# One division of the attention outputs by transposed inverse sums, in place of a division of each row of probabilities

## The chip, the cores and the metric

The kernel runs on one core of a Trainium2 chip. The metric is the time of one execution on the device, in microseconds (us), as the median of several runs. Each engine of the core (TensorE, VectorE, ScalarE, POOL, also called GpSimd, and SyncE, which only issues transfers) takes its own instructions strictly in order and waits for other engines at semaphores.

## The reference

A trunk of two layers works on 512 latent tokens and 256 context tokens of width 1024. Each layer is a modulated norm, one input projection, four groups of four heads ("mixers"), an output projection, and a SwiGLU feed-forward part. Three of the four mixers are softmax attentions: MLA over all latent and context tokens, a two-dimensional neighbourhood attention (NA) and a windowed attention with sink logits (SWA). The fourth is a retention. Context tokens read only context tokens; in the last layer they are not carried on. Cut to what the change concerns:

```python
def softmax_attend(q, k, v, scale, sink=None):
    s = einsum('bhqd,bhkd->bhqk', q, k) * scale
    if sink is not None:
        s = concatenate([s, broadcast(sink)], axis=-1)
    p = softmax(s, axis=-1)
    if sink is not None:
        p = p[..., :-1]
    return einsum('bhqk,bhkd->bhqd', p, v)
```

The softmax divides each row of exponentials by its sum. Since a row's sum is the same for all of its keys, the division may stand before or behind the product with V.

## The kernel before

**Tiling.** Tokens lie in tiles of 128: four latent, two of context. Attention goes by query tile: six tiles per mixer in the first layer and four in the second, so 3 x 6 + 3 x 4 = 30 query tiles of four heads, 120 heads in all. Widths of a head's row of probabilities P are 768 keys in MLA (32 heads), 512 in NA (32), 512 or 640 in SWA (16 of each) and 256 for context tiles (24).

**One head.** TensorE writes the scores into PSUM (`scores`, line 626, and masks). VectorE takes the row's minimum (the scores are negated; line 1000 and 1002 in MLA). ScalarE writes the exponentials to P in SBUF, with the row's sum as a second result (line 1005 in MLA, in two pieces of 384 keys; lines 1148 and 1150 in SWA, line 939 in NA). `norm_p` (lines 595 to 613) adds the pieces of the sum (line 600 or 604), takes the reciprocal (line 607) and multiplies P by it in place on VectorE (line 613). `attend_T` transposes P in blocks of 128 on TensorE (line 579) and copies the result to SBUF, the first four blocks on ScalarE (line 582), the rest on VectorE (line 584). For each pair of heads `attend_pv` then multiplies V by these (line 592). The output of a tile comes out transposed: features on the partitions, queries along the free dimension, the two pairs in columns 0 to 255 of a PSUM bank of the pool "o". `put` (line 620) copies it to SBUF on ScalarE; for MLA, `merge_mla` instead splits it straight from PSUM into two parts, hi on ScalarE and lo on VectorE (lines 1324 and 1325).

**Queries.** `q_stack` loads a tile of queries, transposes it (line 662), and scales it into two tiles, on ScalarE (line 666) and on VectorE (line 667); the scores need both.

**Around it.** Dense products are computed as three matmuls each (`mm3`, lines 467 to 469), of 128x512 columns near the attention. The order of all instructions comes from a list scheduler, which goes by costs and priorities, and puts dense products between the steps of the attention, so TensorE's listing mixes both. Also in the listing near attention: modulation vectors computed from streamed weights (lines 395 and 397, VectorE), the gating and adding of projections (line 1353 on VectorE, 1355 on POOL), the splitting of weights (line 449 on ScalarE, 213 on VectorE or POOL), the retention's decays (lines 1239 and 1263 on VectorE, 1255 on POOL), and, behind attention, the second norm (line 486 on VectorE, transposed by line 500 on TensorE).

## Time and profile before

| | us |
|---|---|
| median of 3 runs | 1928.17 |
| lowest, highest run | 1925.45, 1930.57 |
| the profiled execution | 1927.69 |
| its span, first to last instruction | 1925.9 |
| TensorE busy | 1832.2 |
| VectorE busy | 1196.8 |
| ScalarE busy | 688.9 |
| POOL busy | 614.3 |

The mean granted clock of TensorE is 0.983 of full speed. The attention lies in four stretches: from about 140 to 303 us (context and latent tiles of NA and SWA, first layer), 438 to 530 (MLA, first layer), 1228 to 1337 (NA and SWA, second layer) and 1450 to 1528 (MLA, second layer). To read the profile, take the busy shares first, then the same per stretch, and then what each wait of the busiest engine ended on: only time for which that engine waits, or which it spends itself, can shorten or lengthen the span directly. In the views of time a row's start is followed by its duration; a duration of several instructions in one row runs from the first start to the last end, and durations of matmuls that follow each other overlap, so the step from one start to the next is what the engine pays.

### The profile page before, as it was taken

To read this page: it belongs to the slowest core of one execution; us is meant where nothing else is said; L and a number is where in the kernel's file an instruction comes from. 1 tells how busy PE (TensorE), PEld (TensorE's weight loads), DVE (VectorE), ACT (ScalarE), POOL (GpSimd) and SP (SyncE) were. 2 spreads that over 40 slices of the span, in tenths; PEclk is the share of its full clock that TensorE was granted. 3 is DMA by queue.
4 is the path that set the end of the run, shared out by engine and by line. 5 is a ranking of instruction groups with operands and counts; after the bars stand their busy time and mean duration, and the time that the engine had idled before them with its cause. 6 is when DMAs were issued, how large, how long until landed. Compare 5 with 4: busy or idle time off the path is not lost.

```text
span 1925.9 us, 32215 instructions
## 1 busy us (share of the span) xinstructions
PE 1832.2 (95%) x12367; PEld 1596.9 (83%) x12367; DVE 1196.8 (62%) x2743; ACT 688.9 (36%) x1597; POOL 614.3 (32%) x573
## 2 busy tenths in 40 slices
PE   7899999899999999999999999899889999999997
PEld 3677776778889989999899978678778899999996
DVE  5796886777898776453334283465588854344336
ACT  3325653255542111222122233464255532222223
POOL 0211113223124553444444121111232145636442
PEclk9999999899999999999999999999999999999998
DMA  7665435453124345342222122422434143223321
GB/s 233 209 205 156 139 98 181 133 167 82 61 83 147 111 153 186 110 136 64 62 67 66 54 97 81 119 73 92 138 111 109 34 125 95 88 88 93 105 77 44
DMA packets 193572, 215.48 MB, mean 112 GB/s; under 512 B 66660, under 2 KB 141578, under 8 KB 193418
## 3 DMA queue, kind: packets, MB, share of 16 engines
q10 hardware_dynamic: 75840, 111.17, 18.3%
q1 hardware_dynamic: 117578, 102.25, 18.0%
q8 instruction: 97, 1.59, 0.3%
q14 instruction: 57, 0.47, 0.1%
HBM read 192.76 MB, written 20.63 MB: 111 GB/s over the span
## 4 chain that ended last, share of the span: by engine, by line
PE 65%; DVE 8%; issue 2%; POOL 2%; DMA 1%; ACT 1%; SPq 0%; ACTq 0%; DVEq 0%; POOLq 0%
PE ps L467 10%; PE ps L468 10%; PE ps L469 10%; PE pg L469 8%; PE pg L467 8%; PE pg L468 8%; PE po L592 2%; PE ps L626 2%; PE pt L579 2%; DVE wl L213 1%; DVE nat L1353 1%; DVE PT L397 1%; DVE P L613 1%; DVE b L1239 1%; DMA qT<-in_ada_w_dram 0%
## 5 line engine op out<-in xcount | busy, mean ns | idle before, releaser
L467 PE MATMUL ps<-b,wh 128*128 128x256 f32 x1760 | 501.9, 285 | 3.8 <-ACT P L1464 3.8
L468 PE MATMUL ps<-b,wh 128*128 128x256 f32 x1760 | 500.9, 285 | 0.0
L469 PE MATMUL ps<-b,wl 128*128 128x256 f32 x1760 | 500.3, 284 | 0.4 <-POOL wl L213 0.4
L467 PE MATMUL pg<-wh,b 128*128 128x512 f32 (+2 forms) x1128 | 441.9, 392 | 1.2 <-ACT b L508 0.9
L469 PE MATMUL pg<-wh,b 128*128 128x512 f32 (+2 forms) x1128 | 440.7, 391 | 0.6 <-POOL b L213 0.6
L468 PE MATMUL pg<-wl,b 128*128 128x512 f32 (+2 forms) x1128 | 439.6, 390 | 1.2 <-DVE rs_yn L288 0.6
L467 PEld LDWEIGHTS ps<-b,wh 128*128 128x128 f32 x1760 | 340.1, 193 | 7.1 <-ACT P L1464 4.1
L468 PEld LDWEIGHTS ps<-b,wh 128*128 128x128 f32 x1760 | 340.1, 193 | 0.8
L469 PEld LDWEIGHTS ps<-b,wl 128*128 128x128 f32 x1760 | 340.2, 193 | 0.6 <-POOL wl L213 0.6
L213 DVE TENSOR_TENSOR wl<-raw,wh 128x1024 fp32r<-128x1024 f32 (+1 forms) x130 | 200.8, 1549 | 199.0 <-ACT wh L449 197.8
L449 ACT ACTIVATE wh<-raw 128x1024 fp32r<-128x1024 f32 (+1 forms) x196 | 202.7, 1049 | 256.9 <-PE pg L469 210.4
L1355 POOL TENSOR_TENSOR b<-b,nat 128x512 f32<-128x512 f32 (+1 forms) x204 | 221.3, 1103 | 114.2 <-DVE nat L1353 81.6
L213 POOL TENSOR_TENSOR wl<-raw,wh 128x1024 fp32r<-128x1024 f32 (+1 forms) x66 | 165.9, 2514 | 265.1 <-ACT wh L449 254.3
L467 PEld LDWEIGHTS pg<-wh,b 128*128 128x128 f32 x1128 | 214.4, 190 | 38.9 <-issue 1.7
L469 PEld LDWEIGHTS pg<-wh,b 128*128 128x128 f32 x1128 | 214.2, 190 | 38.9 <-issue 3.9
L468 PEld LDWEIGHTS pg<-wl,b 128*128 128x128 f32 x1128 | 214.1, 190 | 38.1 <-DVE wl L213 1.7
L1353 DVE TENSOR_TENSOR nat<-pg,gate 128x512 f32<-128x512 f32 x240 | 162.0, 686 | 85.6 <-PE pg L469 80.2
L213 POOL TENSOR_TENSOR b<-P,b 128x256 fp32r<-128x256 f32 x36 | 28.9, 804 | 327.3 <-ACT b L1467 327.3
L1467 ACT ACTIVATE b<-P 128x256 fp32r<-128x256 f32 x110 | 45.7, 416 | 233.0 <-DVE P L1466 221.9
L1466 DVE TENSOR_TENSOR P<-ps,P 128x256 f32<-128x256 f32 x110 | 46.4, 422 | 129.6 <-PE ps L469 129.5
L1464 ACT ACTIVATE P<-ps 128x256 f32<-128x256 f32 x110 | 41.5, 383 | 213.4 <-PE ps L469 131.6
L397 DVE SCALAR_TENSOR_TENSOR PT<-qT,consts,PT 128x512 f32<-128x512 f32 x112 | 102.1, 927 | 19.3 <-DMA qT<-in_ada_w_dram 18.4
(322 smaller groups left out, 2446.5 us busy)
## 6 DMA issues: line engine op xcount, KB each, us to landing
raw<-in_ffn_w_dram ACTq DMA_DIRECT2D x132, 512.0 KB
qT<-in_ada_w_dram ACTq DMA_DIRECT2D x96, 256.0 KB
raw<-in_w_in_dram SPq DMA_DIRECT2D x40, 512.0 KB
a<-in_ada_w_dram SPq DMA_DIRECT2D x32, 256.0 KB
a<-in_ada_w_dram ACTq DMA_DIRECT2D x32, 256.0 KB
xn<-in_ada_w_dram ACTq DMA_DIRECT2D x32, 256.0 KB
raw<-in_w_out_dram SPq DMA_DIRECT2D x16, 512.0 KB
ldq<-q_d SPq DMA_DIRECT2D x40, 128.0 KB
```

What stands on the lines that cost most here:

```text
L213: eng.tensor_tensor(out, full, hi.bitcast(F32), op=ALU.subtract)
L397: dve.scalar_tensor_tensor(acc[s], w, sS[:, k, s:s + 1], acc[s], op0=ALU.mult, op1=ALU.add)
L449: act.activation(hi, raw_ap, AF.Copy)
L467: pe.matmul(ps, a[0], b[0], start=first, stop=False)
L468: pe.matmul(ps, a[0], b[1], start=False, stop=False)
L469: pe.matmul(ps, a[1], b[0], start=False, stop=last)
L579: pe.transpose(ps[:, i * P:(i + 1) * P], Pm[:, (b0 + i) * P:(b0 + i + 1) * P], ident)
L1353: dve.tensor_tensor(tm, ps, gates[(0 if t < 4 else 2) + b], op=ALU.mult)
L1355: eng.tensor_tensor(ap, ap, tm[:, a:c], op=ALU.add)
L1464: act.activation(s1[j][:, sl], ps[:, 0:256], AF.Silu)
L1466: dve.tensor_tensor(s1[j][:, sl], ps[:, 0:256], s1[j][:, sl], op=ALU.mult)
L1467: act.activation(gh[j][:, sl], s1[j][:, sl], AF.Copy)
```

## The change

`norm_p` goes, with its three calls in the mixers and the one in `soft_y` (context tiles). P stays undivided. A new function `inverse` is called once per query tile behind the last product with V: it adds the pieces of the sums for all four heads at once (none, one or two additions of 128x4), takes one reciprocal 128x4, spreads it on POOL to 128x256 (each head's inverse 64 times along the free dimension, into a new SBUF tag `rcb` with two buffers), and transposes this in two blocks on TensorE into columns 256 to 511 of the outputs' PSUM bank, where each inverse then stands at the feature and query at which it is needed. `put` copies the transposed inverses to SBUF on ScalarE and multiplies the outputs by them on VectorE. `merge_mla` goes through `put` into a tile `o` first, and splits hi and lo from there.

```diff
--- before.py
+++ after.py
@@ -75,7 +75,7 @@
 
 
 
-CHANGED = {'pad': {'raw': 1024}, 'bufs': {'raw': 4}}
+CHANGED = {'pad': {'raw': 1024, 'rcb': 256}, 'bufs': {'raw': 4, 'rcb': 2}}
 
 
 def merged(opts):
@@ -592,32 +592,32 @@
                 pe.matmul(pv[64 * e:64 * e + 64, hp * P:hp * P + P], vs[e][i], PTs[e][:, i, :],
                           start=(i == n - 1), stop=(i == 0), tile_position=(0, 64 * e))
 
-    def norm_p(Pm, sums):
-
-        n = sums.shape[1]
-        if n == 2:
-            t = S("sm", 1)
-            dve.tensor_tensor(t, sums[:, 0:1], sums[:, 1:2], op=ALU.add)
-            sums = t
-        elif n > 2:
-            t = S("sm", 1)
-            dve.tensor_reduce(t, sums, axis=AX.X, op=ALU.add)
-            sums = t
-        rc = S("rc", 1)
-        dve.reciprocal(rc, sums)
-        e = PNE[rr["pn"] % len(PNE)]
-        rr["pn"] += 1
-        if e == "act":
-            act.activation(Pm, Pm, AF.Copy, scale=rc[:, 0:1])
+    def inverse(pv, sums):
+
+
+        n = sums.shape[2]
+        if n == 1:
+            t = sums[:, :, 0]
         else:
-            {"dve": dve, "pool": pool}[e].tensor_scalar(Pm, Pm, rc[:, 0:1], 1.0, op0=ALU.mult, op1=ALU.mult)
+            t = S("sm", 4)
+            dve.tensor_tensor(t, sums[:, :, 0], sums[:, :, 1], op=ALU.add)
+            if n == 3:
+                dve.tensor_tensor(t, t, sums[:, :, 2], op=ALU.add)
+        rc = S("rc", 4)
+        dve.reciprocal(rc, t)
+        rb = T("rcb", [P, H, 64])
+        pool.tensor_copy(rb, rc.unsqueeze(2).to_broadcast([P, H, 64]))
+        for hp in range(2):
+            pe.transpose(pv[:, 256 + hp * P:384 + hp * P], rb[:, 2 * hp:2 * hp + 2].rearrange("p a b -> p (a b)"), ident)
 
     def put(pv, dst):
 
-        src = pv[:, 0:256].rearrange("p (a b) -> p a b", a=2)
+        rt = T("rcb", [P, 256])
+        act.activation(rt, pv[:, 256:512], AF.Copy)
+        src, r = (x.rearrange("p (a b) -> p a b", a=2) for x in (pv[:, 0:256], rt))
         if len(dst.shape) == 4:
-            src = pv[:, 0:256].rearrange("p (a r c) -> p a r c", a=2, r=8)
-        act.activation(dst, src, AF.Copy)
+            src, r = (x.rearrange("p (a r c) -> p a r c", a=2, r=8) for x in (pv[:, 0:256], rt))
+        dve.tensor_tensor(dst, src, r, op=ALU.mult)
 
     def scores(ps, q, k):
 
@@ -647,9 +647,9 @@
                                accum_out=sums[:, h, 0:1])
                 if negsink is not None:
                     act.activation(sums[:, h, 1:2], m[:, h:h + 1], AF.Exp, bias=sk[:, h:h + 1])
-                norm_p(Pm, sums[:, h, 0:1 if negsink is None else 2])
                 PTs.append(attend_T(Pm, 2))
             attend_pv(pv, hp, PTs, [v_of(2 * hp), v_of(2 * hp + 1)])
+        inverse(pv, sums[:, :, 0:1 if negsink is None else 2])
         return pv
 
     def q_stack(src, scale):
@@ -942,10 +942,10 @@
                             PTs, vs = [], []
                         vs.append([Vw[(2 * cb + b) // 3][:, (2 * cb + b) % 3, dsl] for b in range(2)]
                                   + [Vyn[:, b, dsl] for b in range(2)])
-                        norm_p(Pm, sums[:, h:h + 1])
                         PTs.append(attend_T(Pm, 4))
                         if h % 2:
                             attend_pv(pv, h // 2, PTs, vs)
+                    inverse(pv, sums.unsqueeze(2))
                     put(pv, st[:, :, 0:NX].rearrange("p a (r c) -> p a r c", c=64)[:, :, :, 16 * cb:16 * cb + 16])
                 Q["so"].dma_start(oT_d[0:256, :].rearrange("(a p) t -> p a t", p=P)[:, :, 0:ntok], st[:, :, 0:ntok])
 
@@ -1006,10 +1006,10 @@
                                        accum_out=s2[:, h, i:i + 1])
                     if h % 2 == 0:
                         PTs = []
-                    norm_p(Pm, s2[:, h])
                     PTs.append(attend_T(Pm, 6))
                     if h % 2:
                         attend_pv(pv, h // 2, PTs, [vof(h - 1, range(6)), vof(h, range(6))])
+                inverse(pv, s2)
                 return pv
 
             def k_rope(t):
@@ -1152,10 +1152,10 @@
                             if h % 2 == 0:
                                 PTs = []
                             act.activation(s3[:, h, 2:3], m[:, h:h + 1], AF.Exp, bias=sink[:, l, h:h + 1])
-                            norm_p(Pm, s3[:, h])
                             PTs.append(attend_T(Pm, nl + 2))
                             if h % 2:
                                 attend_pv(pv, h // 2, PTs, [vof(h - 1, blks + [4, 5]), vof(h, blks + [4, 5])])
+                        inverse(pv, s3)
                         o = pv
                     put(o, st[:, :, rows(t)])
                 Q["so"].dma_start(oT_d[256:512, :].rearrange("(a p) t -> p a t", p=P)[:, :, 0:ntok], st[:, :, 0:ntok])
@@ -1320,7 +1320,8 @@
         def merge_mla(t, pv):
             tsl = slice((t % 2) * P, (t % 2) * P + P)
             hi, lo = (x[:, 0:2, tsl] for x in m_pair(t // 2, 0))
-            v = pv[:, 0:256].rearrange("p (a b) -> p a b", a=2)
+            v = T("o", [P, 2, P])
+            put(pv, v)
             act.activation(hi, v, AF.Copy)
             dve.tensor_tensor(lo, v, hi.bitcast(F32), op=ALU.subtract)
```

In the changed program TensorE has 60 matmuls more, VectorE 226 instructions fewer, ScalarE 10 more and POOL 30 more. The scheduler's order outside of the attention stretches and what lies next to them is as before. Three places follow, with the names and line numbers of each program's own listing (the changed file's lines below `put` are those of before plus one).

TensorE before, a latent MLA tile of the first layer, two pieces. The first begins at the fourth head's last scores (`ps_5264`), the second holds that head's transposes (`P_5271`); `pg` are dense products, `pt` the transposes, `po` the outputs.

```order
L626 MATMUL ps_5264<-b_920_4033,qT_5132 128x384
L626 MATMUL ps_5264<-b_920_4033,qT_5133 128x384
L626 MATMUL ps_5264<-b_921_4034,qT_5145 128x384
L467 MATMUL pg_5545<-wh_5304,b_1156_5034 128x512
L468 MATMUL pg_5545<-wl_5305,b_1156_5034 128x512
L469 MATMUL pg_5545<-wh_5304,b_1156_5034 128x512
L579 MATMUL pt_5172<-consts,P_5163 128x128 x4
L579 MATMUL pt_5178<-consts,P_5163 128x128 x2
L467 MATMUL pg_5545<-wh_5304,b_1156_5034 128x512
L468 MATMUL pg_5545<-wl_5305,b_1156_5034 128x512
L469 MATMUL pg_5545<-wh_5304,b_1156_5034 128x512
L467 MATMUL pg_5545<-wh_5310,b_1156_5034 128x512
```

The second piece, 19 rows further down:

```order
L592 MATMUL po_5148<-PT_5171,b_922_4035 64x128
L579 MATMUL pt_5248<-consts,P_5239 128x128 x2
L579 MATMUL pt_5254<-consts,P_5239 128x128 x2
L469 MATMUL pg_5545<-wh_5310,b_1156_5034 128x512
L467 MATMUL pg_5562<-wh_5304,b_1162_5073 128x512
L579 MATMUL pt_5280<-consts,P_5271 128x128 x4
L579 MATMUL pt_5286<-consts,P_5271 128x128 x2
L468 MATMUL pg_5562<-wl_5305,b_1162_5073 128x512
```

Between the two pieces stand dense products, the second and third heads' transposes and the first pair's products with V. TensorE in the changed program, the fourth head of a latent MLA tile of the first layer:

```order
L579 MATMUL pt_5149<-consts,P_5145 128x128 x4
L579 MATMUL pt_5155<-consts,P_5145 128x128 x2
L626 MATMUL ps_5165<-b_891_3954,qT_5061 128x384
L467 MATMUL pg_5252<-wh_5208,b_1124_4946 128x512
L468 MATMUL pg_5252<-wl_5209,b_1124_4946 128x512
L469 MATMUL pg_5252<-wh_5208,b_1124_4946 128x512
L467 MATMUL pg_5252<-wh_5208,b_1124_4946 128x512
L468 MATMUL pg_5252<-wl_5209,b_1124_4946 128x512
L469 MATMUL pg_5252<-wh_5208,b_1124_4946 128x512
L467 MATMUL pg_5252<-wh_5214,b_1124_4946 128x512
L468 MATMUL pg_5252<-wl_5215,b_1124_4946 128x512
L579 MATMUL pt_5176<-consts,P_5172 128x128 x3
```

The scores of the fourth head (`ps_5165`) are now followed by eight dense products and then by its transposes (`P_5172`), which stand in two pieces.

VectorE before, the same tile of before, from the first head's sum on:

```order
L600 TENSOR_TENSOR sm_5166<-s_1179_5149 128x1
L1000 TENSOR_REDUCE m_1200_5226<-ps_5227 128x1
L607 RECIPROCAL rc_5168<-sm_5166 128x1
L1000 TENSOR_REDUCE m_1200_5226<-ps_5232 128x1
L613 TENSOR_SCALAR P_5163<-P_5163,rc_5168 128x768
L600 TENSOR_TENSOR sm_5198<-s_1179_5149 128x1
L1002 TENSOR_TENSOR m_1203_5237<-m_1200_5226 128x1
L1000 TENSOR_REDUCE m_1210_5258<-ps_5259 128x1
L607 RECIPROCAL rc_5200<-sm_5198 128x1
L1000 TENSOR_REDUCE m_1210_5258<-ps_5264 128x1
L584 COPY PT_5171<-pt_5178 128x256
L613 TENSOR_SCALAR P_5195<-P_5195,rc_5200 128x768
```

VectorE in the changed program, the tile shown of it above, from the first pair's copies to the product in `put`:

```order
L1002 TENSOR_TENSOR m_1169_5143<-m_1166_5132 128x1
L1000 TENSOR_REDUCE m_1174_5159<-ps_5160 128x1
L584 COPY PT_5148<-pt_5155 128x256
L1000 TENSOR_REDUCE m_1174_5159<-ps_5165 128x1
L1002 TENSOR_TENSOR m_1177_5170<-m_1174_5159 128x1
L603 TENSOR_TENSOR sm_5198<-s_1149_5065 128x4
L607 RECIPROCAL rc_5200<-sm_5198 128x4
L584 COPY PT_5175<-pt_5182 128x256
L1354 TENSOR_TENSOR nat_5265<-pg_5252,gate_4798 128x512
L620 TENSOR_TENSOR o_5269<-po_5064,rcb_5270 128x256
```

Additions, reciprocals and scalings between the reductions are gone; one addition and one reciprocal of four columns stand behind the last minimum, and the product (line 620) behind a dense product's gating.

VectorE before, near 153 us, between the first and the second context tile of NA in the first layer; line 395 takes a streamed weight (`xn`), line 639 reduces context scores:

```order
L613 TENSOR_SCALAR P_1394<-P_1394,rc_1396 128x256
L395 TENSOR_SCALAR ldr_3057<-xn_3042,consts 128x512
L667 SCALAR_TENSOR_TENSOR qT_1418<-pt_1412,qT_1417 128x512
L676 TENSOR_TENSOR nat_1992<-pg_1965,nat_1992 128x2x64
L1109 COPY b_453_1964<-pg_1965 128x128
L397 SCALAR_TENSOR_TENSOR ldr_3057<-xn_3045,consts,ldr_3057 128x512
L639 TENSOR_REDUCE m_296_1423<-ps_1424 128x2
L639 TENSOR_REDUCE m_296_1423<-ps_1454 128x2
```

and in the changed program:

```order
L1109 COPY b_447_1940<-pg_1941 128x128
L667 SCALAR_TENSOR_TENSOR qT_1414<-pt_1408,qT_1413 128x512
L395 TENSOR_SCALAR ldr_2977<-xn_2962,consts 128x512
L620 TENSOR_TENSOR st_1332<-po_1345,rcb_1402 128x2x128
L639 TENSOR_REDUCE m_295_1419<-ps_1420 128x2
L639 TENSOR_REDUCE m_295_1419<-ps_1444 128x2
L397 SCALAR_TENSOR_TENSOR ldr_2977<-xn_2965,consts,ldr_2977 128x512
L607 RECIPROCAL rc_1468<-s_294_1418 128x4
```

The scaled queries (line 667) stood behind line 395 and now stand ahead of it; the reductions of the scores stand behind it in both. TensorE in the changed program, where a tile ends: the last product with V, the two transposes of the inverses (line 611), and the queries of a next tile.

```order
L592 MATMUL po_5064<-PT_5175,b_892_3955 64x128
L592 MATMUL po_5064<-PT_5148,b_892_3955 64x128
L611 MATMUL po_5064<-consts,rcb_5202 128x128 x2
L662 MATMUL pt_5278<-consts,ldq_5275 128x128 x4
L982 MATMUL pt_5291<-consts,ldq_5287 96x128 x4
L467 MATMUL pg_5441<-wh_5208,b_1124_4946 128x512
L626 MATMUL ps_5302<-b_887_3950,qT_5283 128x384
L626 MATMUL ps_5307<-b_887_3950,qT_5283 128x384
```

The two transposes stand directly behind the last product with V in all 30 tiles.

## Rows read from the trace of the kernel before

**Rows 1.** The page, busy time, share of the span, instructions.

```profile
PE 1832.2 (95%) x12367; PEld 1596.9 (83%) x12367; DVE 1196.8 (62%) x2743; ACT 688.9 (36%) x1597; POOL 614.3 (32%) x573
```

**Rows 2.** Busy time by stretch: the sum of the four attention stretches; behind the first's end.

```profile
sum 442.00, PE 429.56 PEld 349.24 DVE 338.45 ACT 250.62 POOL 72.68; mean PE 107.39 PEld 87.31 DVE 84.61 ACT 62.65 POOL 18.17
...
530.00:570.00 40.00, 36.01 (x223) 32.31 (x222) 39.57 (x97) 17.21 (x33) 9.11 (x5) 0.97 0.30 100
```

**Rows 3.** TensorE's waits over the span: total us, times, longest us.

```profile
PE ps L626 <- DVE qT L667: 5.0, 3, 2.7
...
PE pt L500 <- DVE xn L486: 3.7, 2, 2.2
PE pt L579 <- DVE P L613: 3.4, 5, 1.0
...
PE pt L579 <- DVE sm L604: 0.8, 2, 0.4
```

**Rows 4.** TensorE in time, an MLA tile: start us, us, line, operation, count.

```profile
463.50 0.39 PE L467 MATMUL pg<-wh,b 128*128 128x512 f32 x1
463.73 0.39 PE L468 MATMUL pg<-wl,b 128*128 128x512 f32 x1
...
467.54 0.38 PE L579 MATMUL pt<-consts,P 128*128 128x128 f32 x2
467.85 1.53 PE L592 MATMUL po<-PT,b 128*64 128x128 f32 x24
...
470.27 0.82 PE L579 MATMUL pt<-consts,P 128*128 128x128 f32 x6
```

**Rows 5.** Groups by line: count | busy us, mean ns of one | idle before.

```profile
L613 DVE TENSOR_SCALAR P<-P,rc 128x512 f32<-128x512 f32 (+3 forms) x120 | 67.0, 561 | 1.4
L607 DVE RECIPROCAL rc<-sm 128x1 f32<-128x1 f32 x72 | 11.0, 155 | 0.6
L1466 DVE TENSOR_TENSOR P<-ps,P 128x256 f32<-128x256 f32 x110 | 46.4, 422 | 129.6 <-PE ps L469 129.5
...
L620 ACT ACTIVATE st<-po 128x256 f32<-128x256 f32 x20 | 7.7, 385 | 17.3 <-PE po L592 12.7 <-DVE ldr L397 4.6
...
L883 POOL COPY b<-o 128x256 f32<-128x256 f32 x4 | 3.6, 910 | 24.0 <-ACT nat L675 15.1 <-DVE nat L795 6.5 <-DVE o L879 2.3
```

**Rows 6.** VectorE, ScalarE and TensorE in time, from scores to transposes.

```profile
495.17 0.16 DVE L1002 TENSOR_TENSOR m<-m 128x1 f32<-128x1 f32 x1
495.24 0.55 DVE L1000 TENSOR_REDUCE m<-ps 128x1 f32<-128x384 f32 x1
...
495.36 0.58 ACT L1005 ACTIVATE P<-ps,m 128x384 f32<-128x384 f32 x1 [3.21 <-DVE m L1002]
...
495.83 0.16 DVE L1002 TENSOR_TENSOR m<-m 128x1 f32<-128x1 f32 x1
...
495.93 0.57 ACT L1005 ACTIVATE P<-ps,m 128x384 f32<-128x384 f32 x1
...
496.40 0.20 ACT L1005 ACTIVATION_READ_ACCUMULATOR P<-ps,m 128x1 f32 x1
...
498.17 0.85 PE L579 MATMUL pt<-consts,P 128*128 128x128 f32 x6
```

**Rows 7.** VectorE beside POOL in time; the scaling's shortest, median, longest ns.

```profile
328.60 8.31 DVE L1239 SCALAR_TENSOR_TENSOR b<-b,gC,b 64x64 f32<-64x64 f32 x10
...
333.81 2.34 POOL L213 TENSOR_TENSOR wl<-raw,wh 128x1024 fp32r<-128x1024 f32 x1 [0.37 <-ACT wh L449]
...
338.38 1.84 DVE L1239 SCALAR_TENSOR_TENSOR b<-b,gC,b 64x64 f32<-64x64 f32 x6
...
L613 DVE TENSOR_SCALAR P<-P,rc x120: 337/483/1697, 144.5 to 1520.6; 128x512 f32<-128x512 f32 x48, 128x768 f32<-128x768 f32 x32, 128x256 f32<-128x256 f32 x24, 128x640 f32<-128x640 f32 x16
```

**Rows 8.** VectorE and TensorE in time, a load that comes late.

```profile
152.97 0.49 DVE L395 TENSOR_SCALAR ldr<-xn,consts 128x512 f32<-128x512 f32 x1 [6.18 <-DMA xn<-in_ada_w_dram]
...
154.11 1.11 PE L626 MATMUL ps<-b,qT 128*128 128x256 f32 x6 [2.71 <-DVE qT L667]
```

## The prediction, made before the change was run

> **What bounds the kernel now.** I read the busy shares first: TensorE is busy for 95% of the span, VectorE for 62% [rows 1]. Then the same by stretch. In the four stretches that hold the attention (the summed row) TensorE works 429.56 of 442 us and VectorE 338.45, or 77% [rows 2]. TensorE has 12.4 us of idle time there, and lighter work on another engine can give back no more than that in those stretches, but for the clock.
>
> Next come TensorE's waits by line, to see how much of this idle time the divided rows of probabilities cause [rows 3]. The transposes of P (line 579) waited 3.4 us for the scaling of line 613 and 0.8 us for the sums of line 604: 4.2 us. The scores (line 626) waited 5.0 us for VectorE's half of the scaled queries (line 667), at three places, 2.7 us of it at one. Behind the first layer's attention the transposes of line 500 waited 3.7 us for line 486; VectorE is busy 39.57 of 40 us there [rows 2, 3]. So VectorE loses work worth far more than the time that TensorE ever waited for it.
>
> **What the change removes.** Line 613 took 67.0 us in 120 instructions, and the reciprocals are 120 of about 0.155 us, 18.6 us [rows 5]; 72 small additions and reductions of the sums go too. That is over 85 us of VectorE time, nearly all of it beside TensorE's work. On TensorE's path lay the 4.2 us of waits, so the gain there is 4.2 at most, and I take all of it. The chain from a head's scores to its transposes gets shorter as well. Its legs [rows 6]: a reduction to the minimum behind it, 495.83 - 495.24 = 0.59; a minimum to its first exponential, 495.36 - 495.17 = 0.19; the first exponential to the second, 495.93 - 495.36 = 0.57; the second to the end of its accumulator's read, 496.60 - 495.93 = 0.67; and from there through addition, reciprocal and scaling to the transposes, 498.17 - 496.60 = 1.57. This last leg goes.
>
> **What it adds.** *TensorE.* Sixty transposes 128x128, two for each of 30 query tiles. One more in a row costs (0.82 - 0.38) / 4 = 0.11 us, from the groups of six and of two [rows 4]: 60 x 0.11 = 6.6 us, and TensorE has nothing to lay them beside. The bounds are this, and nothing where they fall into time in which TensorE would wait anyway; since it waits 12.4 us in 442, I take 6.6. The Trainium skill, "TensorE: Matmul & The Clock Gate", Part 4: PE-mode transpose, puts a transpose at about 275 ns inside a kernel; the trace agrees for the duration of one (0.38 less a step of 0.11 is 0.27), and by it the term would be 16.5 us, but six in a row do not take six durations.
>
> *VectorE.* Thirty products of 128x256 with PSUM as one input, as line 1466 at 0.422 us [rows 5], 12.7 us; 30 reciprocals at about 0.16 and 26 additions at about as much: 22 us in all, against over 85 removed. *ScalarE.* Thirty copies of the transposed inverses at line 620's 0.385 us [rows 5]; twenty stand where line 620 stood, ten are new, 3.9 us, beside TensorE's work. *POOL.* Thirty broadcast copies 128x256; the nearest row is line 883's copy at 0.91 us [rows 5], 27 us in all. This copy is the new wait: addition 0.16, reciprocal 0.16 and copy 0.91 stand between the tile's last exponential and the two transposes, 1.2 us. Behind that exponential TensorE has the fourth head's six transposes, 0.82, a wait for their copies to SBUF, and the second pair's products with V, 1.53 [rows 4]: over 2.3 us. So the copy is hidden as long as POOL is free, and if it is not, the wait holds up the dense products queued behind the transposes on TensorE. For the places where POOL is in a long instruction (2.34 us of line 213 [rows 7]) I count 1 us; the bounds are 0 and 30 x 0.91 = 27.
>
> *Outputs.* Their PSUM bank comes free one copy and one product later, 0.385 + 0.422 = 0.8 us, with the next tile's scores and exponentials still to come before anyone needs it: nothing. In the MLA part the split into hi and lo now waits for the product; ten tiles at 0.8 us are 8 us if the output projection stood right behind, but dense work stands between: nothing.
>
> **What it moves.** The order is a scheduler's, and with the scaling gone it sets less other work between a head's scores and its transposes. Take the fourth head of a latent MLA tile of the first layer. Before, the time from the first instruction behind its scores to its transposes is 470.27 - 463.50 = 6.8 us [rows 4]; the chain needs one matmul's duration, 0.39 [rows 4], then 0.59 + 0.19 + 0.57 + 0.67 + 1.57 [rows 6], together 3.98. The slack is 2.8 us. In the changed order eight dense products stand there, 8 x (463.73 - 463.50) = 1.84 us, and the score's own step, about three quarters of one dense step: 2.0 us. The first three transposes now need the first exponential only, 0.39 + 0.59 + 0.19 + 0.67 = 1.84 us; the fourth comes 0.56 us later and needs 0.57 more. The slack is 0.17 us. A single operation queued ahead on VectorE or ScalarE, such as another head's reduction (up to 0.59), makes TensorE wait 0.4 us. So the waits that go come back under another name, as transposes that wait for ScalarE's exponentials. About two heads in four stand this tightly in the 16 latent MLA and SWA tiles, 32 heads; neighbourhood heads have more room. With something queued at half of them the new waits are 32 x 0.5 x 0.4 = 6.4 us, and 7 with the rest. The bounds are 0, if nothing is ever queued, and 64 heads x 0.35 = 22.
>
> The waits on line 667 change in part. At the largest place VectorE itself had waited 6.18 us for a load in front of line 395, and line 667 stood behind it [rows 8]. In the changed order line 667 stands ahead there, but the reductions of the scores still stand behind line 395, so I let this stall move rather than go. Of the other two places, 5.0 - 2.7 = 2.3 us, I take 1.5 as gained; the bounds for all are 0 and 5.0. The waits on line 486 lie behind attention, where order and load stay: 0, at best 3.7.
>
> **Sum.** 1927.7 (the profiled execution, 0.5 under the median of the runs, 1928.2) + 6.6 - 4.2 - 1.5 + 7 + 1 = 1936.6; the forecast is 1936, slower by 0.4%. A measurement of this kernel can tell about 0.3%, or 5.8 us, from no change: 1922.4 and 1934.0 are the limits.
>
> **Rivals.** *One: the new waits do not come.* The slack suffices because VectorE's queue is shorter: its load in the attention falls from 77% by some 65 of 442 us to about 62%. 1927.7 + 6.6 - 4.2 - 1.5 + 1 = 1929.6, no difference. Against it: the chain consists of operations that stay as long as they are, and lost 1.57 us where its cover lost 4.8.
>
> *Two: VectorE was the hidden bound; faster.* All waits on lines 579, 667 and 486 go, 4.2 + 5.0 + 3.7 = 12.9 us, against 6.6 for the transposes: 1921.4. It comes out so only while new waits of every kind stay under 1 us. For it speaks the stretch with 39.57 busy us of 40 [rows 2]; against it, that this work remains, and that one of the waits is a transfer's.
>
> *Three: the new waits reach their bound.* 1936.6 + 15 = 1951.6. It needs something queued in front of nearly every MLA and SWA head's chain, as where three reductions in a row delay the first exponential.
>
> *Four: POOL and VectorE hold each other up.* While POOL ran line 213 for 2.34 us, ten small VectorE operations took 8.31 us where six took 1.84 soon after, and the longest scaling took 1697 ns against a median of 483 [rows 7]. If a third of the thirty copies stop VectorE where TensorE waits for it, that is 10 x 0.91 = 9 us more: 1946. The Trainium skill, "SBUF — State Buffer", Who interferes with whom, says that the two engines lock each other out of a shared pair of ports for a whole instruction, and the long rows agree; by it the scalings that go would also stop holding up POOL, so the rule cuts both ways.
>
> **How the numbers follow.** Forecast, 1934 to 1944: 0.43. Rival one, 1923 to 1934: 0.30. Rival two: 0.13. Rival three: 0.07. Rival four: 0.07. The range leaves out half of rival two and the far ends of three and four: 1921 to 1948. Faster 0.13; the same 0.30; slower 0.57.
>
> **What would show it.** In the changed trace line 579 should wait for the exponentials (lines 1005 and 1148 before) by 5 to 10 us over the attention, where nothing stood; the wait on line 613 must be gone; the sixty transposes should come in steps of 0.11 us behind the last product with V, without a wait for POOL; VectorE should be busy some 65 us less. If the waits on the exponentials stay away, rival one is right; if those on line 486 or the transfer's stall go too, rival two; if the inverses' transposes wait for POOL by more than 5 us, or VectorE's operations beside POOL's copies stretch, rival four.

## The result, and the profile after

The changed kernel took 1945.85 us (median of four runs, 1942.69 to 1946.75) against 1929.37 us of the kernel before beside it: a ratio of 1.0079, 95% interval 1.0060 to 1.0099. It is slower by 16.5 us, in the direction forecast and about twice as far (1936). The profiled execution has a span of 1945.0 us; that of before had 1925.9.

One sentence of the section on the change was wrong: in the changed file only the lines behind `merge_mla` are one more (line 1465 answers 1464, 1356 answers 1355); lines 620 to 1320 keep their numbers.

The page's busy line and the sum of the same four stretches, which answer [rows 1] and [rows 2]:

```profile
PE 1848.2 (95%) x12427; PEld 1605.3 (83%) x12427; DVE 1147.2 (59%) x2517; ACT 690.0 (35%) x1607; POOL 626.8 (32%) x603
```

```profile
1228.00:1337.00 109.00, 100.31 (x763) 80.71 (x761) 51.30 (x152) 60.39 (x170) 16.68 (x17) 0.97 0.24 71
...
sum 442.00, PE 420.19 PEld 337.88 DVE 269.77 ACT 246.88 POOL 88.00; mean PE 105.05 PEld 84.47 DVE 67.44 ACT 61.72 POOL 22.00
```

These windows are at the times of before, and the changed program stands later in them by 0 to 21 us, so they catch other work: the summed row has less TensorE work than before, and its VectorE row (338.45 to 269.77) and the clock of 0.97 in the third stretch can't be set against those of before directly. In windows moved along with the work (140 to 308, 444 to 540, 1244 to 1353 and 1468 to 1547 us) TensorE works 439.26 of 452 us, the share of before (97%), VectorE 280.96, some 57 us less, and the granted clock is 0.99 to 1.00. Over the span VectorE lost 50 us. TensorE is busy 16.0 us more over the span, of a growth of 19.1; its idle time hardly moved (93.7 to 96.8 us).

The new groups (count | busy us, mean ns | idle before), beside [rows 5]: the transposes of the inverses, their copy to SBUF, the product, and the broadcast copy.

```profile
L611 PE MATMUL po<-consts,rcb 128*128 128x128 f32 x60 | 13.1, 301 | 0.0
```

```profile
L616 ACT ACTIVATE rcb<-po 128x256 f32<-128x256 f32 x30 | 11.5, 384 | 37.9 <-PE po L611 35.7 <-DMA qT<-in_ada_w_dram 2.1
```

```profile
L620 DVE TENSOR_TENSOR st<-po,rcb 128x256 f32<-128x256 f32 x20 | 8.5, 424 | 18.4 <-ACT rcb L616 18.3
```

```profile
L609 POOL COPY rcb<-rc 128x256 f32<-128x256 f32 x30 | 12.8, 425 | 203.4 <-DVE rc L607 190.1 <-PE pt L579 12.4 <-DMA ldq<-q_d 0.9
```

Where a tile of MLA ends on TensorE (start, duration), the two transposes stand behind the last product with V as in the listing:

```profile
476.10 1.53 PE L592 MATMUL po<-PT,b 128*64 128x128 f32 x24
477.56 0.44 PE L611 MATMUL po<-consts,rcb 128*128 128x128 f32 x2
477.84 0.60 PE L662 MATMUL pt<-consts,ldq 128*128 128x128 f32 x4
```

Two transposes take 477.84 - 477.56 = 0.28 us from start to start here. Added up over all sixty in the same way they took 6.69 us, and no idle time of TensorE ahead of them is listed but for 0.2 us ahead of one of their weight loads, behind POOL.

TensorE's waits over the span, the rows that answer [rows 3] and the larger new ones (total us, times, longest):

```profile
PE pu L686 <- DVE st L620: 3.5, 1, 3.5
...
PE pt L500 <- DVE xn L486: 2.5, 2, 1.8
PE pu L404 <- DVE ldr L397: 2.4, 1, 2.4
PE pu L404 <- ACT P L1465: 2.3, 1, 2.3
...
PE pt L579 <- ACT P L1148: 1.0, 1, 1.0
...
PE pt L579 <- ACT P L646: 0.5, 1, 0.5
PE ps L928 <- ACT qT L666: 0.5, 1, 0.5
...
PE ps L1136 <- DVE qT L667: 0.5, 1, 0.5
...
PE ps L929 <- DVE qT L667: 0.4, 1, 0.4
PE pt L579 <- ACT P L1005: 0.4, 1, 0.4
...
PE ps L626 <- ACT qT L666: 0.4, 1, 0.4
...
PE pt L579 <- ACT P L939: 0.3, 1, 0.3
```

The waits on the scaling (line 613) and on the sums are gone, and waits on exponentials (lines 1148, 646, 1005, 939) stand in their place, 2.2 us of them. The 5.0 us behind line 667 fell to 0.9, but 3.5 us stand at line 686 instead, and 0.9 at the scaled queries' other half, ScalarE's (line 666), where before had none. In time (VectorE, then TensorE), answering [rows 8]:

```profile
155.38 0.48 DVE L395 TENSOR_SCALAR ldr<-xn,consts 128x512 f32<-128x512 f32 x1 [4.14 <-DMA xn<-in_ada_w_dram]
155.78 0.42 DVE L620 TENSOR_TENSOR st<-po,rcb 128x256 f32<-128x256 f32 x1
...
156.25 0.44 PE L686 MATMUL pu<-consts,nat 128*128 128x128 f32 x2 [3.50 <-DVE st L620]
```

The late load still holds VectorE in front of line 395; what stands behind it in VectorE's order is now the new product of `put`, and TensorE waits until VectorE has come past it.

Time between the same instructions in both profiles tells where the 19 us arose (times of before; worked out from the starts of the instructions that both have):

| stretch of before | what it holds | longer by, us |
|---|---|---|
| 20 to 135 | start | 0.1 |
| 135 to 437 | NA, SWA, retention, first layer | 5.5 |
| 437 to 571 | MLA and the second norm, first layer | 4.8 |
| 571 to 1155 | feed-forward, first layer | 5.5 |
| 1155 to 1450 | NA, SWA, retention, second layer | 2.4 |
| 1450 to 1562 | MLA, second layer | 1.1 |

Over a quarter of it lies in the feed-forward part, in which the change touches nothing and the order is the same.

### The profile page after: what moved, and what is told of

It is laid out like the page before. It is cut to its first block, busy times and chain, and to the rows that moved or that the text cites. A ratio compares the mean times of both kernels' runs of the same rounds, so it can differ in the third digit from the quotient of the medians.

```text
span 1945.0 us, 32160 instructions
## 1 busy us (share of the span) xinstructions
PE 1848.2 (95%) x12427; PEld 1605.3 (83%) x12427; DVE 1147.2 (59%) x2517; ACT 690.0 (35%) x1607; POOL 626.8 (32%) x603
## 3 DMA queue, kind: packets, MB, share of 16 engines
q10 hardware_dynamic: 75840, 111.17, 18.1%
## 4 chain that ended last, share of the span: by engine, by line
PE 60%; DVE 7%; ACT 1%; POOL 1%; issue 1%; DMA 1%; SPq 0%; ACTq 0%; DVEq 0%; POOLq 0%
PE ps L467 10%; PE ps L468 10%; PE ps L469 10%; PE pg L469 7%; PE pg L467 7%; PE pg L468 7%; PE po L592 1%; DVE wl L213 1%; PE pt L579 1%; PE ps L626 1%; DVE b L213 1%; DVE ldq L507 1%; DVE b L1356 1%; DVE nat L1354 1%; DVE b L1239 1%
## 5 line engine op out<-in xcount | busy, mean ns | idle before, releaser
L213 DVE TENSOR_TENSOR wl<-raw,wh 128x1024 fp32r<-128x1024 f32 (+1 forms) x130 | 204.7, 1581 | 208.0 <-ACT wh L449 207.9
L397 DVE SCALAR_TENSOR_TENSOR PT<-qT,consts,PT 128x512 f32<-128x512 f32 x112 | 99.7, 908 | 14.8 <-DMA qT<-in_ada_w_dram 13.8
```

The source lines that it names most:

```text
L213: eng.tensor_tensor(out, full, hi.bitcast(F32), op=ALU.subtract)
L397: dve.scalar_tensor_tensor(acc[s], w, sS[:, k, s:s + 1], acc[s], op0=ALU.mult, op1=ALU.add)
```

## The experiments

All twelve stand beside runs of the kernel before on their own chip; ratios are to these. As the executions of one kernel spread over several us, I also compare means over all executions: 1930.7 us for the kernel before (59 executions, 1924.4 to 1936.4), and 1944.0 for the changed one (10, with the first experiment's), so 13.3 us apart.

### The changed kernel again

No edit.

> The changed kernel once more. Theory A (the cost sits on TensorE's path: 6.7 us of transposes, and waits that follow from the order, the same in every execution): 1.008 of before, spread of the executions under 2 us, and the same waits in the profile. Theory B (a part is decided anew in each execution by who comes first, VectorE or POOL): the long splitting of weights on VectorE in the feed-forward part (6.4 us instead of 1.2 to 2.1), three times after and twice before in the profiles so far, comes another number of times, each time worth 2 to 4 us, and the executions spread over 4 us or more.

Measured: 1942.09 us median (1937.22 to 1948.55), ratio 1.0062 [1.0039, 1.0085]; theory B's spread. The feed-forward stretch was 2.6 us longer than in the profile of before, not 5.5. The long splittings of weights came four times in it, not three. What they are, in the first changed profile (VectorE, POOL, TensorE):

```profile
835.68 6.39 DVE L213 TENSOR_TENSOR wl<-raw,wh 128x1024 fp32r<-128x1024 f32 x1
...
835.95 1.99 POOL L1356 TENSOR_TENSOR b<-b,nat 128x512 f32<-128x512 f32 x2
837.89 0.75 POOL L1356 TENSOR_TENSOR ldr<-ldr,nat 128x256 f32<-128x256 f32 x1
838.58 2.40 POOL L213 TENSOR_TENSOR wl<-raw,wh 128x1024 fp32r<-128x1024 f32 x1
...
843.02 0.66 PE L404 MATMUL pu<-PT,consts 128*32 128x128 f32 x8 [2.30 <-ACT P L1465]
```

and at the same place in the profile of before:

```profile
823.48 1.41 DVE L213 TENSOR_TENSOR wl<-raw,wh 128x1024 fp32r<-128x1024 f32 x1
...
823.75 2.99 POOL L1355 TENSOR_TENSOR b<-b,nat 128x512 f32<-128x512 f32 x2
```

VectorE's and POOL's instructions start 12.20 us later in the first than in the second, both of them, to 0.01 us. In the one VectorE's operation ends at 842.07 us, 1.1 us behind the last that POOL had queued (838.58 + 2.40 = 840.98); in the other VectorE's is done in 1.41 us and POOL's two last 1 us longer. The Trainium skill, "SBUF — State Buffer", Who interferes with whom, says that whichever of the two engines issues first holds the shared ports for the whole instruction, and the other is blocked; the trace agrees that one blocks the other, and differs in that here the block lasted for a chain of POOL's instructions. The collision at this place stands in 11 of the 14 profiles of this study, and not in that of before. TensorE's wait of 2.30 us, with 3.4 us at the lower clock behind it, came with 3.7 us of the difference between the two profiles. That this is the luck of an execution and not of the change is likely, as both outcomes follow the same starts, but it is not shown: the kernel before was profiled once, so how often it falls which way there is not known.

### Removal alone, and addition alone

Removal: `norm_p` gone, `put` and `merge_mla` as before.

```diff
     def inverse(pv, sums):
-        n = sums.shape[2]
...
+        pass
     def put(pv, dst):
...
-        dve.tensor_tensor(dst, src, r, op=ALU.mult)
+        act.activation(dst, src, AF.Copy)
```

> Only the division of P goes; nothing divides the outputs (the division by the sums is left out). Theory A: without the transposes (6.7 us) and without the product's wait behind a late load (3.7 us) the changed kernel's 1946 falls to about 1935, still not under before, as waits on the exponentials (about 6.7 us) stand where waits on the scaling stood. Rival (VectorE's relief is worth something by itself): under 1922.

Measured: 1937.75 us, ratio 1.0028 [1.0013, 1.0043]; by means 5.4 us slower than before. VectorE was busy 66 us less:

```profile
PE 1837.2 (95%) x12367; PEld 1596.0 (83%) x12367; DVE 1130.6 (58%) x2431; ACT 686.1 (35%) x1597; POOL 611.2 (32%) x573
```

So VectorE's relief, with nothing else added, gave no gain in this order. The rival falls. The waits on exponentials were 6.0 us here (the lines are those of this kernel):

```profile
PE pt L579 <- ACT P L630: 3.6, 2, 3.0
...
PE pt L579 <- ACT P L989: 1.4, 2, 1.1
...
PE pt L579 <- ACT P L1132: 1.0, 1, 1.0
```

against 4.2 us of waits on scaling and sums before [rows 3]: the exchange that was forecast.

Addition: P is divided as before, and the outputs once more.

```diff
+                        norm_p(Pm, sums[:, h:h + 1])
                         PTs.append(attend_T(Pm, 4))
...
                     inverse(pv, sums.unsqueeze(2))
```

> P is divided as before, and the outputs are divided a second time by the inverses (divides twice): only the addition is made. Theory A: before plus 6.7 us of transposes plus the product's wait of up to 3.7: 1936 to 1940, with the waits on the scaling as before (about 7 us). Rival (removal of the scaling makes the loss, by the tighter order): the addition alone costs the transposes at most, under 1937, and the removal alone about 10 us.

Measured: 1942.59 us, ratio 1.0057 [1.0036, 1.0077], 12.0 us over before by means: above theory A's 1936 to 1940 and above the rival's bound. Its sixty transposes took 7.7 us from start to start, and its waits on the scaling were 5.2. Addition and removal sum to 17 us, where the whole is 13.

### Without the transposes

```diff
-        for hp in range(2):
-            pe.transpose(pv[:, 256 + hp * P:384 + hp * P], ...)
...
-        act.activation(rt, pv[:, 256:512], AF.Copy)
+        act.activation(rt, pv[:, 0:256], AF.Copy)
```

> The changed kernel without the sixty transposes; the outputs are multiplied by themselves instead of the inverses, all else stays. Theory A: 6.7 us less than the changed kernel, 1939 against 1946. Rival (the transposes fall into time in which TensorE waits): no difference to the changed kernel, within 2 us. Theory B: the difference is anything between -4 and 14, since the order moves as well.

Measured: 1925.37 us, ratio 0.9971 [0.9958, 0.9985]: faster than before by 4.6 us in the means, and 18 us under the changed kernel, where theory A said 6.7. It has all of the rest, the broadcast copies, ScalarE's copies and the products, but nothing waits for the broadcast copies any more, so the chain of `put` is shorter too. It is also 10 us under the removal alone, which does less work on three engines. A mechanism that counts only work on TensorE and the waits between the same neighbours can't give that. The two differ in the scheduler's order: by line, names and shape in the traces, 1014 of TensorE's 12367 common instructions stand elsewhere than in the changed kernel, 550 in the removal alone.

### One part at a time

In the MLA part alone (10 tiles), and in NA and SWA alone (20 tiles); the other part keeps `norm_p` and the plain copy.

```diff
-                PTs.append(attend_T(Pm, 2))
+                if not inv:
+                    norm_p(Pm, sums[:, h, 0:1 if negsink is None else 2])
+                PTs.append(attend_T(Pm, 2))
...
+        if inv:
+            inverse(pv, sums[:, :, 0:1 if negsink is None else 2])
```

> The change in the MLA part alone (10 query tiles, 20 transposes); NA and SWA divide P as before. If the costs add up by place, as the stretches of the changed trace have them (MLA and what follows it, 437 to 571 and 1450 to 1562: about 6 us), 1937; transposes alone would make 1933. If the order decides (the scheduler's whole order moves with any edit), anything from 1926 to 1942, without relation to the 20 transposes.

Measured: 1929.29 us, ratio 0.9998 [0.9985, 1.0012], although its 20 transposes took 2.5 us.

> The change in NA and SWA alone (20 query tiles, 40 transposes); MLA divides P as before. By place (135 to 437 and 1217 to 1450: 8 us of the changed profile, and 4.4 of them transposes) 1939; with the part in the MLA alone the two should sum to the whole, 11 to 16 us. If the order decides: 1926 to 1942, and the two don't sum.

Measured: 1937.48 us, ratio 1.0035 [1.0021, 1.0049]; its 40 transposes took 4.3 us. The two parts sum to 5.4 us by means, the whole is 13.3. The MLA stretch, 4.8 us longer in both profiles of the changed kernel, was 0.2 us shorter in the one that changes MLA only. The costs don't add up by place.

### The broadcast on VectorE

```diff
-        pool.tensor_copy(rb, rc.unsqueeze(2).to_broadcast([P, H, 64]))
+        dve.tensor_copy(rb, rc.unsqueeze(2).to_broadcast([P, H, 64]))
```

> The changed kernel with the broadcast copies of the inverses on VectorE instead of POOL, nearly the same order on TensorE. If POOL's copies hold up VectorE or the transposes (rival four), 3 to 6 us faster than the changed kernel, 1937 to 1940; if they are hidden, as the changed trace has it (0.1 us of waiting at the inverses' transposes), the same as the changed kernel within 2 us, 1942 to 1946.

Measured: 1946.38 us, ratio 1.0084 [1.0067, 1.0101], 2.7 us over the changed kernel by means, not under it. The order is nearly that of the changed kernel (135 instructions of TensorE elsewhere, counted in the same way). POOL's copies are not what costs the time; rival four falls for them.

### More transposes

```diff
-        for hp in range(2):
+        for hp in (0, 1, 0, 1):
```

> The changed kernel with each transpose of the inverses made twice, 120 instead of 60. If a transpose's price is its step of 0.11 us on TensorE's path, 6.7 us more than the changed kernel, 1950. If what mattered in the run without transposes (17 us less for 60 fewer) is a price of 0.28 us each, 1960. If it was the order that the scheduler found, between 1938 and 1955.

Measured: 1946.2 us, ratio 1.0083 [1.0065, 1.0101]. The 120 transposes took 13.3 us from start to start, twice the 6.7, and the mean rose by 2.4 us only. The order differs by 817 instructions; in this one the first layer's MLA stretch, with twice the transposes, was 1.1 us longer than before, where the changed kernel's was 4.8.

### The same order, and the same work in other orders

The last four use a plain matmul with w columns of the identity in place of the transposes, and multiply the outputs by themselves, so that nothing reads what it writes.

```diff
-            pe.transpose(pv[:, 256 + hp * P:384 + hp * P], rb[...], ident)
+            pe.matmul(pv[:, 256 + 128 * hp:256 + w + 128 * hp], rb[...], ident[:, 0:w],
+                      start=True, stop=True)
```

With w = 64 the scheduler's order is the changed kernel's in every instruction of TensorE and VectorE.

> The changed kernel with 64 instead of 128 columns in each of the sixty matmuls that transpose the inverses, and the outputs multiplied by themselves; the order of every engine is that of the changed kernel, instruction by instruction. If a transpose costs its step on TensorE's path, half of 6.7 us is saved: 3.3 us under the changed kernel (1944 in the mean of its ten executions), 1940 to 1941. If the path price is larger (0.28 us each), 8 us: 1936. If they lie in waiting time, no difference.

Measured: 1949.54 us, ratio 1.0094 [1.0078, 1.0109]; 4.7 us over the changed kernel by means, where I had expected 3.3 us under it. The edit did not do what I meant: the trace has 120 entries for the sixty matmuls, so such a matmul goes in two passes where the transpose goes in one, and each pass takes as long with 64 columns as with 128. From start to start they took 14.3 us, 7.6 more than the transposes. Read so, the run is the doubled price in an unchanged order: 7.6 us more on TensorE, 4.7 more in the mean, so in this order the time rose with the added work, though not by all of it.

The other three carry the same price (14.0 to 14.9 us) in three other orders, so the less work that their expectations count for fewer columns was not there. Nor did ScalarE's copy run free of them: in the traces of the four it sat idle for 41.6 to 46.7 us behind line 611, in the changed kernel for 35.7, so the chain of `put` is kept.

> Sixty matmuls of 128 columns as in the changed kernel, but ScalarE's copy doesn't wait for them (the outputs are multiplied by themselves); the work is the same and the scheduler's order another, some 1600 of TensorE's 11593 instructions stand elsewhere. If work and its waits decide: 1942 to 1946. If the order that the scheduler finds decides a part: anywhere from 1930 to 1950, at least 4 us from the changed kernel.

> As the last, with 112 columns (0.8 us less work on TensorE in all) and a third order, some 1500 instructions elsewhere. Work: 1941 to 1945. Order: anywhere from 1930 to 1950; the scatter of the runs of this call is then the size of what the order decides.

> As the last two, with 32 columns (5.0 us less work on TensorE than the changed kernel) and a fourth order, some 1700 instructions elsewhere. Work: 1939. Order: 1925 to 1945; under 1930 would be as fast as the run without transposes, with sixty matmuls still in place.

Measured: 1945.46 us (1.0089 [1.0064, 1.0114]), 1944.84 (1.0071 [1.0053, 1.0089]) and 1955.89 (1.0118 [1.0093, 1.0142]); means 1947.0, 1944.3 and 1953.3. By their steps all three would lie 7 to 8 us over the changed kernel's mean, at 1951 to 1952. The one with the fewest columns is the slowest; its six executions fall in two groups, 1945.4 and 1946.3, and 1955.9 to 1958.5, and the profiled one is of the slower group. A tile's end in it, and the group:

```profile
481.34 1.53 PE L592 MATMUL po<-PT,b 128*64 128x128 f32 x24
482.80 0.63 PE L611 MATMUL po<-consts,rcb 128*128 128x32 f32 x4
483.27 0.42 PE L663 MATMUL pt<-consts,ldq 128*128 128x128 f32 x2
```

```profile
L611 PE MATMUL po<-consts,rcb 128*128 128x32 f32 x120 | 19.0, 281 | 0.3 <-POOL rcb L609 0.3
```

Four passes of 32 columns take 483.27 - 482.80 = 0.47 us. In this run's profile the feed-forward stretch alone was 10.6 us longer than in that of before, in the same order there: five long operations of line 213 (VectorE) beside POOL's backlog where before had two, the longest being

```profile
622.49 9.07 DVE L213 TENSOR_TENSOR wl<-raw,wh 128x1024 fp32r<-128x1024 f32 x1
```

and TensorE's waits behind line 1466 (1464 before), 8.8 us where before had 3.8:

```profile
PE ps L467 <- ACT P L1466: 8.8, 2, 4.4
```

So with like work the means scatter over 9 us. In the profiled execution 10.6 us arose far behind the attention, where VectorE and POOL meet, and the slower group, four of six executions of one order, lies about 11 us above the other two; so the 9 us need not be the order's alone.

### The runs side by side

Means of all executions, less 1930.7, less the added matmuls' own steps on TensorE (from each profile):

| run | over before | matmuls' steps | the rest |
|---|---|---|---|
| changed kernel (10 executions) | 13.3 | 6.7 | 6.6 |
| removal alone | 5.4 | 0 | 5.4 |
| addition alone | 12.0 | 7.7 | 4.3 |
| without transposes | -4.6 | 0 | -4.6 |
| MLA only | -0.6 | 2.5 | -3.1 |
| NA and SWA only | 6.0 | 4.3 | 1.7 |
| broadcast on VectorE | 16.0 | 6.6 | 9.4 |
| four transposes | 15.7 | 13.3 | 2.4 |
| w = 64, same order | 18.0 | 14.3 | 3.7 |
| w = 128 | 16.3 | 14.9 | 1.4 |
| w = 112 | 13.6 | 14.8 | -1.2 |
| w = 32 | 22.6 | 14.0 | 8.6 |

The time follows the steps of the added matmuls in the main; what is left lies between -4.6 and 9.4 and goes neither with VectorE's load nor with the number of transposes. No run without the scalings shows a gain that this scatter doesn't cover. No version that computes the reference beat the kernel before: the part in the MLA alone ties with it.

The profiles show where the rest lies. Split each span by TensorE's steps, from one start to the next, less the listed idle time, and compare each step with the median step of the same line and shape before at the higher of the two clock levels (2.4 GHz). What is over, less the same of before, in us (an estimate from single profiles; the parts add up to the span within 0.7, and the 7.7 above of the addition held 0.5 of idle time):

| run | span over before | added matmuls | steps at the higher level | steps at the lower level | idle |
|---|---|---|---|---|---|
| changed kernel | 19.1 | 6.7 | 3.2 | 6.1 | 3.3 |
| changed kernel again | 14.9 | 6.7 | 3.1 | 3.7 | 1.8 |
| removal alone | 7.8 | 0 | 3.8 | 1.1 | 3.0 |
| addition alone | 18.1 | 7.3 | -1.6 | 4.0 | 8.8 |
| without transposes | -0.9 | 0 | 0.1 | 1.6 | -1.9 |
| broadcast on VectorE | 16.8 | 6.6 | 3.8 | 2.0 | 4.4 |
| four transposes | 22.0 | 13.3 | -0.5 | 3.3 | 5.9 |
| w = 64, same order | 21.9 | 14.3 | 3.5 | 2.5 | 1.5 |
| w = 32 | 30.8 | 14.0 | 0.4 | 9.3 | 6.9 |

The steps at the higher level go with the order: 3.1 to 3.8 us in the four profiles that have the changed kernel's order or nearly it, -1.6 to 3.8 in the others. The lower level and the idle time move from execution to execution as well (first two rows). Of the 8.7 us between removal alone and the run without transposes, 3.7 are such steps and 4.9 idle time.

One part of these steps comes with the removal itself. Without the scaling the scores (line 626) of MLA stand directly in front of transposes or products with V at 29 places, where before had 2. In time, from the changed kernel:

```profile
480.52 0.86 PE L626 MATMUL ps<-b,qT 128*128 128x384 f32 x4
481.23 0.39 PE L469 MATMUL pg<-wh,b 128*128 128x512 f32 x1
...
484.58 0.42 PE L626 MATMUL ps<-b,qT 128*128 128x384 f32 x1
484.84 0.55 PE L579 MATMUL pt<-consts,P 128*128 128x128 f32 x3
```

Four scores in a row take (481.23 - 480.52) / 4 = 0.18 us each; the one in front of the transposes takes 0.26, and the view of waits lists nothing there, as the modelled end of a matmul lies behind the next start. Line 626 costs 3.3 to 4.2 us more than before in every profile without the scaling in MLA, and 0.4 more at most in the two that keep it there. In the changed kernel shorter steps of the transposes and queries (lines 579 and 662), 3.6 us in sum, take most of it back.

## Why the prediction was right, and where it was not

**The bound held.** TensorE is 95% busy in both, and VectorE's relief shortened nothing: the removal alone, which takes 66 us from VectorE, was slower by 5.4 us. VectorE's load fell by 50 us over the span where the forecast had 65: durations overlap the next start (line 613 is 67.0 us by durations and 59.5 by steps), and line 213 took 6.9 us more.

**The transposes' term held**: 6.6 us forecast, 6.69 measured from start to start, in the open on TensorE as said. The figure of the Trainium skill ("TensorE: Matmul & The Clock Gate", Part 4: PE-mode transpose), 275 ns, is for bf16; these fp32 transposes come near it in duration alone (301 ns in the mean), and 16.5 us for the sixty, an estimate from that figure, is not what the steps show.

**The waits on the scaling went** (4.2 us), as forecast. **The new waits on exponentials came, but the term was too large** in the changed kernel: 2.2 us by the view of waits where the sum had 7. The step that failed is "something queued at half of them": the listed waits are four, so the slack of 0.17 us sufficed at most of the heads, or what it lacked lies in the longer steps of the scores shown above, which the runs don't tell apart. In the order of the removal alone the same waits were 6.0 us, near the forecast; so the kind of wait was right and its size belongs to the order, which the listing of one place didn't settle.

**The late load's stall moved, as said**, 5.0 us at line 667 before, and 0.9 there and 3.5 at line 686 after: a gain of 0.6 where I had 1.5, and none with the 0.9 behind line 666. I had looked for it behind the reductions; it was the new product in `put` that stood next in VectorE's queue.

**POOL's copy** is hidden (0.2 us of waiting, forecast 1), and takes 425 ns, half of the row I had priced it by. That row mixes one copy that ran alone, 398 ns, with three of 902 to 1389 ns beside VectorE's operations.

**What the sum lacked.** With these measured terms it would have been 6.7 - 4.2 + 2.2 - 0.6 + 0.2 = 4.3 us. The measured 13.3 (means) or 16.5 (first medians) has 9 to 12 us more. So the direction was forecast from a sound term, the transposes, but that the time lies in the range, twice as far from before as forecast, is in good part luck: over half of the difference is made by terms that the sum had at nothing. Of these, the profiles show: one collision of VectorE and POOL in the feed-forward part (3.7 us between the two profiles); waits in work that the change doesn't touch, as 2.4 us at line 404 behind line 397, where before had 0.2; some 6 us by steps at the lower of TensorE's two clock levels (1.2 GHz), at which it stood for 61 us against 55, the last 10 us of either span left out; and 3.2 us of longer steps at the higher level. I had taken the order outside of the listed places to cost nothing. The runs show that it does not: removal alone and the run without transposes lie 10 us apart in their means of twelve executions, and the one with more work is the faster. Which part of the changed kernel's 6.6 us of rest belongs to its order, and which to the longer chain of `put`, is left open in part. The longer steps belong to the order: removal alone has them without that chain (3.8 us), and the runs with four transposes and with w = 32 lack them with it (-0.5 and 0.4). For the waits and the lower clock level no run separates the two, as every edit that would do so moved the order as well.

**The rivals.** One (new waits absent, 1929.6): the waits were small and the time still rose, so it failed on the terms that it shares with the sum. Two (faster): refuted by the removal alone; its 3.7 us at line 500 were besides not all behind the first layer's attention, 2.2 of them stood there and the rest behind the second's. Three (waits at their bound): its time came near, its mechanism not. Four (POOL): refuted for the copies by the run with the broadcast on VectorE; the mechanism that it names was found at work in the feed-forward part instead, between operations that both kernels have. Its row of 8.31 us [rows 7] runs beside five POOL operations and not the one of 2.34 us alone.

## What to carry to other kernels

Take work off an engine only where the busiest one waits for it: 66 us less on VectorE gave nothing here, while the 6.7 us of added steps on TensorE stood in the open. On a program that a scheduler orders, price an edit as its own work on the busiest engine plus a scatter of the order and of the execution, and measure that scatter by variants of like work before believing a difference under 0.5%. Two single profiles can differ by several us through collisions far from the edit; look where the time arose before explaining it.

## What the runs showed of the hardware beyond this

A plain fp32 matmul with the identity takes two passes where a transpose takes one (120 entries for 60), and a pass took about 0.12 us from start to start with 32 columns as with 128 (14.0 and 14.9 us for 120), each with its own weights of 128x128. A VectorE operation on two SBUF inputs that met POOL's backlog lasted 6.4 to 9.4 us instead of 1.4, in the case shown until 1.1 us after POOL's queue was empty. A POOL copy that spreads 4 columns to 256 took 425 ns, a plain copy of that size 398 ns when it ran alone; the mean of 910 [rows 5] comes from copies beside VectorE's operations.
